# A decoder trunk on one core: q and k tokens-first, attention's operands by way of DRAM, norm's quarters in turns

## The chip, the core and the metric

One core of one Trainium2 chip runs the whole kernel as one launch. The metric is the device time of an execution in microseconds (us). The engines are PE (TensorE, matmuls and transposes), DVE (VectorE), ACT (ScalarE), POOL (GpSimd) and SP (SyncE, which here issues every DMA). The engines run their own lists of instructions in order and wait for each other by semaphores.

## The reference

```
h = RMSNorm(x);  p = h @ W_in            # x: 1024 tokens x 1024, float32
gate_pre, a_in, a_z, b_uv, b_z, q, k, v, c_z, f_pre = split(p)
A: a = GLU(a_in); causal depthwise conv, width 31; LayerNorm; silu;  a = a * silu(a_z);  y_a = a @ w_a
B: u, v = split(b_uv); v = RMSNorm(v); per group of channels tril(W_s) @ v + b_s, chunks of 128;
   y = u * mixed * silu(b_z);  y_b = y @ w_b
C: q, k = RMSNorm per head (64 wide, 8 heads); logf = log_sigmoid(f_pre + b_f); c = cumsum(logf)
   s = q k^T / 8 + c_i - c_j, causal; softmax; o = p @ v;  o = o * silu(c_z);  y_c = o @ w_c
g = sigmoid(gate_pre + b_gate)           # three of 1024 channels
out = x + (g_a*y_a + g_b*y_b + g_c*y_c) @ W_out
```

## The kernel before

Every product of float32 operands is made of three matmuls on parts: an operand is split into hi (a rounded copy) and lo (the rest), and hi·hi, lo·hi and hi·lo are added in PSUM. So each operand needs a cast (mostly ACT) and a subtraction (DVE or POOL).

The stages in order:

1. **V.** Eight tiles of 128 tokens. norm makes a tile of h, trans transposes it on PE (tile tp, line 365) and splits it (h_hi on ACT, h_lo on DVE), prod multiplies it with the weights of v and f (tiles pa and pb, lines 385 and 386) and copies the result to v and fz. The steps of the tiles are woven by hand, so that the transposes of tile i+1 stand inside the products of tile i.
2. **GLU and mixing.** Slabs of 128 output channels, features-first: slab loads 2 x 256 KB of a weight (raw), splits it (w_hi on ACT at line 147, w_lo on DVE or POOL at line 148), and gemm_steps does two halves of 512 tokens, 24 matmuls each (line 160), and hands each half's PSUM tile to an evac function. Mixing is branch B's part over tokens (lines 541 and 558).
3. **Attention.** For eight heads, scores are made per block of 128 queries (score), their weights transposed (turned) and multiplied with v (weigh). Between these small pieces stand fillers: fill(n) takes n steps from a queue of slabs. Before, the queue holds q and k of the next pair of heads (qk_steps, with the statistics matmuls at lines 206 and 207 some steps later), slabs of gates and slabs of u. ready(h) builds a head's operands from q, k and v in SBUF with casts on ACT and DVE and subtractions on POOL. The taps of branch A's convolution (tile acc, line 268) are dealt out over DVE between all this (pace and TAPS).
4. **Tail.** gated slabs (a silu gate times a branch's output, then hi and lo into br), merge slabs (merge_steps, which multiply br with w_c, w_b or w_a and with a gate gt that was stored before attention's end), branch A's LayerNorm in four quarters of 256 tokens (norm_steps), and last the product with W_out.

PE's order is the order of the code (a manual schedule for TensorE). On ACT, DVE, POOL and SP a scheduler sets the order from priorities: slab runs at raised priority, score, turned and weigh at another.

A function of another table set on ACT is preceded by an ACT_TABLE_LOAD in ACT's list.

Of the kernel before, what the change touches and what calls it, by code (L numbers as in the profile page):

```python
# [33 lines left out]
def trunk_kernel(ctx, tc, x, norm_g, w_in, b_gate, conv_w, conv_b, conv_norm_g, conv_norm_b,  # L34
# [55 lines left out]
    vo_ctx, vo = pool("vo", bufs=JC, side="right")  # L90
    vp = [vo.tile([P, NT, P], F32, name=f"v{p}", tag="vo") for p in range(JC)]
# [95 lines left out]
    def qk_steps(c0, gcol, res):  # L187
        w = slab(w2, KC, c0)
        qn = prep.tile([P, S], F32, name="qn", bufs=2)
        res.append(qn)  # L190

        def evac(hf, ps, ts):
            raw = qn[:, ts]
            sq = prep.tile([P, HALF], F32, name="sq")
            hi = prep.tile([P, HALF], F32R, name="sqhi")
            lo = prep.tile([P, HALF], F32R, name="sqlo")
            nc.scalar.copy(raw, ps)
            nc.scalar.activation(hi, ps, AF.Square)
            nc.scalar.activation(sq, ps, AF.Square)
            nc.vector.tensor_tensor(lo, sq, f32(hi), op=ALU.subtract)  # L200

            def stat():
                y0 = prep.tile([P, HALF], F32, name="y0")
                s2 = prep.tile([P, HALF], F32, name="s2")
                st = stp.tile([P, HALF], F32, name="st", tag="st")
                nc.tensor.matmul(st, lhsT=ones_hd, rhs=hi, start=True, stop=False)
                nc.tensor.matmul(st, lhsT=ones_hd, rhs=lo, start=False, stop=True)
                rsqrt(None, st, y0, s2, s2)
                nc.gpsimd.tensor_tensor(raw, raw, y0, op=ALU.mult)
                nc.vector.scalar_tensor_tensor(raw, raw, vec[:, gcol:gcol + 1], s2,  # L210
                                               op0=ALU.mult, op1=ALU.mult)

            later.append([7, stat])

        yield from gemm_steps(w, hT, evac)
# [800 lines left out]
```

## Time and profile before

| what | value |
|---|---|
| three runs | 1080.76, 1084.75 (median), 1085.66 us |
| the profiled execution | 1080.82 us, its span 1078.9 us |
| instructions | 14403 |
| PE busy | 1063.1 us, 99% of the span |
| DVE, ACT, POOL busy | 668.4, 461.1, 315.8 us |
| granted clock of TensorE | 1.00 of full speed, 0.99 in the last stage |

The span is the time between the first and the last record of the profile; the execution's time is that and what lies around it. The busy time of PE counts matmuls whose ends are modelled and overlap the next, so its share is no measure of how close PE is to its peak. What PE loses is read from its waits and from the starts of its matmuls.

### The profile page before, as it was taken

What the parts mean: (1) busy time and instruction counts of PE and PEld (TensorE: products, weight loads), DVE (VectorE), ACT (ScalarE), POOL (GpSimd) and SP (SyncE); (2) the same over time, 40 slices, a digit from 0 to 9 for tenths busy, and PEclk for the clock granted to TensorE, in tenths of its full rate; (3) what the DMA queues carried; (4) which work ended last, traced back from release to release, by engine and by line L of the source; (5) the groups of instructions that cost most, each with busy time, mean ns of one, the idle gap of its engine ahead of it and who ended that gap; (6) DMA issues with size and microseconds to landing.
All of it is one profiled execution on the core that took longest, in us unless ns stands there. A gap on an engine that the chain in (4) does not pass through costs nothing.

```text
span 1078.9 us, 14403 instructions
## 1 busy us (share of the span) xinstructions
PE 1063.1 (99%) x5256; PEld 894.9 (83%) x5256; DVE 668.4 (62%) x1233; ACT 461.1 (43%) x877; POOL 315.8 (29%) x297
## 2 busy tenths in 40 slices
PE   8999999999999899999999999999999999999998
PEld 7988888888878788888887888878888888888887
DVE  7557797878587858885788563335654355387111
ACT  6431124524366444754574444346766332365000
POOL 0022321214665646575657564201100000000000
PEclk9999999999999999999999999999999999999999
DMA  9213321023322232132222322132355233372321
GB/s 302 84 30 100 91 75 40 21 69 88 98 59 69 75 102 67 47 104 88 60 59 79 88 87 89 32 92 68 100 155 161 77 128 108 98 246 96 108 98 59
DMA packets 109443, 99.72 MB, mean 92 GB/s; under 512 B 7406, under 2 KB 82198, under 8 KB 109373
## 3 DMA queue, kind: packets, MB, share of 16 engines
q1 hardware_dynamic: 109372, 98.81, 29.9%
q8 instruction: 41, 0.67, 0.3%
q14 instruction: 30, 0.24, 0.1%
HBM read 76.21 MB, written 22.58 MB: 92 GB/s over the span
## 4 chain that ended last, share of the span: by engine, by line
PE 88%; DVE 5%; DMA 3%; ACT 1%; POOL 1%; issue 1%; SPq 0%; ACTq 0%; POOLq 0%; DVEq 0%
PE ps L160 63%; PE ops L958 8%; PE tv L541 4%; PE o L690 3%; PE tpp L670 2%; DVE acc L268 2%; PE s L647 1%; PE s L648 1%; PE pa L385 1%; PE pb L386 1%; DMA raw<-in_w_in_dram 1%; PE pm L558 1%; DVE sqlo L200 1%; DMA xt<-in_x_dram 1%; DMA mixT<-in_w_in_dram 0%
## 5 line engine op out<-in xcount | busy, mean ns | idle before, releaser
L160 PE MATMUL ps<-h_hi,w_hi 128*128 128x512 f32 x896 | 357.1, 399 | 0.9 <-DVE mixT L699 0.9
L160 PE MATMUL ps<-h_hi,w_lo 128*128 128x512 f32 x896 | 350.3, 391 | 3.3 <-POOL w_lo L148 3.3
L160 PE MATMUL ps<-h_lo,w_hi 128*128 128x512 f32 x896 | 349.6, 390 | 0.0
L268 DVE SCALAR_TENSOR_TENSOR acc<-a_in,cwT,acc 128x512 f32<-128x512 f32 x240 | 236.7, 986 | 3.8
L160 PEld LDWEIGHTS ps<-h_hi,w_lo 128*128 128x128 f32 x896 | 168.2, 188 | 40.3 <-POOL w_lo L148 3.8
L160 PEld LDWEIGHTS ps<-h_hi,w_hi 128*128 128x128 f32 x896 | 168.3, 188 | 31.2 <-ACT w_hi L147 1.3
L160 PEld LDWEIGHTS ps<-h_lo,w_hi 128*128 128x128 f32 x896 | 168.6, 188 | 30.0
L148 POOL TENSOR_TENSOR w_lo<-raw,w_hi 128x512 fp32r<-128x512 f32 x82 | 117.2, 1430 | 144.3 <-ACT w_hi L147 140.7
L147 ACT CAST w_hi<-raw 128x512 fp32r<-128x512 f32 x136 | 83.9, 617 | 143.4 <-PE ps L160 110.5
L160 PE MATMUL ps<-br,w_hi 128*128 128x512 f32 x384 | 118.3, 389 | 0.0
L676 DVE TENSOR_TENSOR plo<-tpp,phi 128x512 fp32r<-128x512 f32 (+1 forms) x80 | 50.7, 633 | 73.7 <-ACT phi L675 73.7
L160 PEld LDWEIGHTS ps<-br,w_hi 128*128 128x128 f32 x384 | 71.9, 188 | 14.7
L160 PE MATMUL ps<-br,w_lo 128*128 128x512 f32 x192 | 74.7, 389 | 0.0
L656 ACT ACTIVATE pt<-pt,nm 128x1024 f32<-128x1024 f32 (+3 forms) x64 | 49.8, 778 | 48.3 <-DVE nm L651 48.1
L148 DVE TENSOR_TENSOR w_lo<-raw,w_hi 128x512 fp32r<-128x512 f32 x54 | 37.3, 690 | 53.4 <-ACT w_hi L147 53.0
L640 POOL TENSOR_TENSOR cb<-cb,mask 128x128 f32<-128x128 f32 x64 | 44.0, 688 | 85.7 <-DVE nm L651 78.3
L659 POOL TENSOR_SCALAR pt<-pt,nm 128x1024 f32<-128x1024 f32 (+3 forms) x64 | 54.3, 848 | 49.3 <-DVE nm L658 48.9
L675 ACT CAST phi<-tpp 128x512 fp32r<-128x512 f32 (+1 forms) x80 | 43.4, 543 | 56.5 <-PE tpp L670 56.2
L966 DVE SCALAR_TENSOR_TENSOR xr<-ops,xr 128x512 f32<-128x512 f32 (+1 forms) x17 | 11.2, 660 | 72.3 <-PE ops L958 67.5
L807 ACT ACTIVATE gt<-gt,vec 128x512 f32<-128x512 f32 x46 | 32.9, 723 | 46.6 <-DMA gt<-gpre 40.4
L958 PE MATMUL ops<-wo_lo,mhi 128*128 128x512 f32 (+1 forms) x136 | 51.2, 377 | 0.0
L958 PE MATMUL ops<-wo_hi,mlo 128*128 128x512 f32 (+1 forms) x136 | 51.2, 376 | 0.0
(200 smaller groups left out, 1628.4 us busy)
## 6 DMA issues: line engine op xcount, KB each, us to landing
raw<-in_w_in_dram SPq DMA_DIRECT2D x112, 256.0 KB, 2.9
gpre<-gst SPq DMA_DIRECT2D x46, 256.0 KB, 2.0
gt<-gpre SPq DMA_DIRECT2D x46, 256.0 KB, 2.8
xt<-in_x_dram SPq DMA_DIRECT2D x8, 512.0 KB, 4.0
cb<-cT_d SPq DMA_DIRECT2D x16, 256.0 KB, 3.5
wo_raw<-in_w_out_dram SPq DMA_DIRECT2D x16, 256.0 KB, 2.7
xr<-in_x_dram SPq DMA_DIRECT2D x15, 256.0 KB, 3.7
out_dram<-xr SPq DMA_DIRECT2D x15, 256.0 KB, 2.0
```

What stands on the lines that cost most here:

```text
L147: nc.scalar.copy(hi, raw)
L148: lo_eng[0].tensor_tensor(lo, raw, f32(hi), op=ALU.subtract)
L160: nc.tensor.matmul(ps, lhsT=wk[a][:, k, :], rhs=act[b][kc][:, ts], start=kc == 0 and n == 0, stop=kc == len(w) * KH - 1 and n == 2)
L268: nc.vector.scalar_tensor_tensor(acc, a_in[:, k:k + HALF], cwT[:, j, k:k + 1], acc, op0=ALU.mult, op1=ALU.add)
L541: nc.tensor.matmul(tv, lhsT=a[:, kc, ts], rhs=b[kc][:, 0:DB], start=kc == 0 and n == 0, stop=kc == KC - 1 and n == 2)
L640: nc.gpsimd.tensor_tensor(cb[:, own], cb[:, own], mask, op=ALU.add)
L656: nc.scalar.activation(pt[:, 0:kl_], pt[:, 0:kl_], AF.Exp, bias=nm[:, ci:ci + 1], scale=-1.0, accum_out=nm[:, 2:3])
L659: ins = nc.gpsimd.tensor_scalar(pt[:, 0:kl_], pt[:, 0:kl_], nm[:, 3:4], 1.0, op0=ALU.mult, op1=ALU.mult)
L675: nc.scalar.copy(phi[:, 1:n + 1], tp[:, 0:n])
L676: ins = nc.vector.tensor_tensor(plo[:, 1:n + 1], tp[:, 0:n], f32(phi[:, 1:n + 1]), op=ALU.subtract)
L807: nc.scalar.activation(dst[hf], dst[hf], AF.Tanh, bias=bias, scale=0.5)
L958: nc.tensor.matmul(ps, lhsT=a[kc][:, ts], rhs=b[:, kc, c:c + cols], start=kc == 0 and n == 0, stop=kc == KC - 1 and n == 2)
```

## The change

- q and k are made tokens-first in 8 + 8 tiles (qk_tile) behind the first and second GLU slab: 24 matmuls into pq, RMS statistics over each head's 64 columns on ACT and DVE, the product on DVE, four transposes on PE two tiles later, hi and lo, and a store of each to DRAM. The weights of q and k are loaded and split as those of v are (weights).
- v is split in the V stage (tile vt) and stored to DRAM, one tile later than it was copied before.
- ready(h) loads a head's operands with six DMAs into tiles whose pools are open from the first stage on. It has no work on ACT, DVE or POOL.
- Attention's filler queue holds 21 gate slabs, six slabs of silu inputs (z_pre, stored to DRAM), four slabs of u and two more gates. The gaps and taps per place, and the number of score buffers (two to three), change.
- In the tail the six z slabs are read back (gated_pre, no matmuls), norm's quarters run two in turn, and merge_steps takes its weight ahead of its gate, whose tanh is issued behind the weight's cast.

```diff
-GAPS = (5, 5, 5, 5, 5, 5, 5, 5, 4, 12)
-TAPS = (3, 3, 3, 3, 2, 2, 2, 2, 0, 0)
+GAPS = (5, 5, 5, 5, 5, 6, 6, 6, 5, 5)
+TAPS = (2, 2, 2, 2, 2, 1, 1, 1, 1, 1)
-NPRE = sum(PLAN)
+NPRE = 23
+ZPRE = [(1, 0), (1, 1), (0, 0), (0, 1), (0, 2), (0, 3)]
...
-    def qk_steps(c0, gcol, res):
-        w = slab(w2, KC, c0)
...
+    def z_pre(bi, j):
+        def evac(hf, ps, ts):
+            st = prep.tile([P, HALF], F32, name="gst", bufs=2)
+            nc.scalar.copy(st, ps)
+            nc.sync.dma_start(out=zpre[bi, j][:, ts], in_=st)
+
+        yield from gemm_steps(slab(w2, KC, Z0[bi] + j * P), hT, evac)
...
+    def ready(h):
+
+        e, p = h % 2, h // 2
+        own, oth = slice(e * HD, (e + 1) * HD), slice((1 - e) * HD, (2 - e) * HD)
+        ka = stk.tile([P, S], F32R, name="ka")
+        qa = stk.tile([P, S], F32R, name="qa")
+        vc = stk.tile([P, NT, 2 * HD], F32R, name="vc")
+        with tc.high_priority(offset=PRIO):
+            for t, rows, src in ((qa, own, qk_d[0][0]), (qa, oth, qk_d[0][1]), (ka, own, qk_d[1][0]),
+                                  (ka, oth, qk_d[1][0]), (kls[e], own, qk_d[1][1])):
+                nc.sync.dma_start(out=f32(t[rows]), in_=src[own, p, :])
+            nc.sync.dma_start(out=f32(vc), in_=v_d[:, :, 2 * h * HD:2 * (h + 1) * HD])
...
-            for p in range(JC):
-                src = (pa, pb)[p // 2][:, (p % 2) * P:(p % 2 + 1) * P]
-                (nc.scalar.copy if p % 2 else nc.vector.tensor_copy)(vp[p][:, i, :], src)
+            yield
+            vt = stk.tile([P, NH, 2, HD], F32R, name="vt", tag="vc")
             nc.vector.tensor_tensor(fz[:, i, :], pb[:, N1:N1 + NH], bfb, op=ALU.add)
+            for n, src in enumerate((pa, pb)):
+                hs = slice(n * NH // 2, (n + 1) * NH // 2)
+                src = src[:, 0:N1].rearrange("p (h d) -> p h d", d=HD)
+                nc.scalar.copy(vt[:, hs, 0, :], src)
+                nc.vector.tensor_tensor(vt[:, hs, 1, :], src, f32(vt[:, hs, 0, :]), op=ALU.subtract)
+            nc.sync.dma_start(out=v_d[:, i, :], in_=f32(vt).rearrange("p h b d -> p (h b d)"))
             yield
+        def qk_tile(i, w, gcol, dst):
+
+            ts = slice(i * P, (i + 1) * P)
+            pq = ps0.tile([P, HALF], F32, name="pq", tag="pa", bufs=2)
+            for kc in range(KC):
+                for n, (a, b) in enumerate(((h_hi, w.hi), (h_lo, w.hi), (h_hi, w.lo))):
+                    nc.tensor.matmul(pq, lhsT=a[:, kc, ts], rhs=b[kc][:, 0:DC],
+                                     start=kc == 0 and n == 0, stop=kc == KC - 1 and n == 2)
+                if kc == KC // 2 - 1:
+                    yield
+            sqn = stk.tile([P, 2, NH, HD], F32, name="sqn", tag="qa")
+            sq, qn = sqn[:, 0], sqn[:, 1]
+            r = p0x.tile([P, 4, NH], F32, name="qr")
+            nc.scalar.activation(sq, pq.rearrange("p (h d) -> p h d", d=HD), AF.Square, scale=float(HD) ** -0.5)
+            nc.vector.tensor_reduce(r[:, 3], sq, axis=mybir.AxisListType.X, op=ALU.add)
+            rsqrt(r[:, 2], r[:, 3], r[:, 0], r[:, 1], r[:, 2])
+            nc.vector.tensor_tensor(qn, pq.rearrange("p (h d) -> p h d", d=HD),
+                                    r[:, 2].unsqueeze(2).broadcast_to([P, NH, HD]), op=ALU.mult)
+            yield
...
+            nc.scalar.activation(hi, tp, AF.Copy, scale=gain)
+            ins = nc.vector.scalar_tensor_tensor(lo, tp, gain, f32(hi), op0=ALU.mult, op1=ALU.subtract)
+            for t, d in zip((hi, lo), dst):
+                nc.sync.dma_start(out=d[:, :, ts], in_=f32(t))
+            pace(ins, 3)
+            yield
...
-        queue += [glu_steps(j) for j in range(JA)]
+        queue += [glu_steps(0)]
...
+        wq = weights(Q0)
...
+        fill(1000)
+        queue += [glu_steps(1)]
+        qk_tiles(wq, 36, qk_d[0])
+        wk = weights(K0)
...
+        queue += [glu_steps(j) for j in range(2, JA)]
+        qk_tiles(wk, 37, qk_d[1])
+        ready(0)
...
-        queue += [gate_pre(next(gates)) for _ in range(PLAN[1])]
-        fill(7)
-        ready(0)
-        fill(14)
+        fill(8)
         early(score, 0, 3, 1)
...
+    def gated_pre(dst, bi, j, src):
+
+        for b in dst:
+            b.append(br.tile([P, S], F32R, name="br", tag="br"))
+        for hf in range(NHALF):
+            ts = slice(hf * HALF, (hf + 1) * HALF)
+            z = zp.tile([P, HALF], F32, name="z")
+            nc.sync.dma_start(out=z, in_=zpre[bi, j][:, ts])
+            a = src(hf, ts)
+            nc.scalar.activation(z, z, AF.Silu)
+            nc.vector.tensor_tensor(a, a, z, op=ALU.mult)
+            nc.scalar.copy(dst[0][j][:, ts], a)
+            nc.vector.tensor_tensor(dst[1][j][:, ts], a, f32(dst[0][j][:, ts]), op=ALU.subtract)
...
-                nc.scalar.activation(dst[hf], dst[hf], AF.Tanh, bias=bias, scale=0.5)
+                with tc.issue_after(hi_ins[0].ins):
+                    nc.scalar.activation(dst[hf], dst[hf], AF.Tanh, bias=bias, scale=0.5)
...
     def merge_steps(bi, d, b, wm, gt=None, after=None):
+        w = slab(wm[0], len(b[0]), d * P)
...
-    queue += [gated(bb, j, BZ0, lambda hf, ts, j=j: mixT[:, j, ts]) for j in range(2)]
     queue += [merge_steps(2, d, cc, w_c) for d in range(KC)]
...
-        for q in range(S // QT):
-            for _ in norm_steps(q):
-                fill(16)
+        quarters = [norm_steps(q) for q in range(S // QT)]
+        for turn_ in ((0,), (1,), (0,), (1,), (0, 2), (1, 3), (2,), (3,), (2,), (3,)):
+            for q in turn_:
+                next(quarters[q], 0)
+            if turn_[0] < 2 and len(turn_) > 1:
+                j = turn_[0]
+                gated_pre(bb, 1, j, lambda hf, ts, j=j: mixT[:, j, ts])
+            fill(14)
```

How the lists of instructions stand in the two built programs is shown at three places. A line is source line, operation, output <- inputs and shape; lines of the changed kernel have that kernel's own line numbers.

The first place is DVE in the V stage, from the hi and lo split of a tile of h (h_lo) to the next norm's product (xt). Before:

```order
L368 TENSOR_TENSOR h_lo<-tp,h_hi 128x4x128 x2
L391 COPY v_84<-pa 128x128
L391 COPY v_86<-pb 128x128
L392 TENSOR_TENSOR fz<-pb,bfb 128x8
L121 TENSOR_TENSOR r<-r 128x1
L122 SCALAR_TENSOR_TENSOR r<-r 128x1
```

With the change:

```order
L375 TENSOR_TENSOR h_lo<-tp,h_hi 128x4x128 x2
L398 TENSOR_TENSOR fz<-pb,bfb 128x8
L403 TENSOR_TENSOR vt<-pa,vt 128x4x64
L403 TENSOR_TENSOR vt<-pb,vt 128x4x64
L125 TENSOR_TENSOR r<-r 128x1
L126 SCALAR_TENSOR_TENSOR r<-r 128x1
```

Two copies have become two subtractions on 128 x 256, and pa and pb are here those of the tile before the one that PE is at: PE's first matmul on pa of the tile after waits for the first L403, its first on pb for the second.

The second place is ACT in the tail, where the last cc slab ends (z_7196 and br_7105 before, z_7646 and br_7527 with the change are its second half; st2 is a norm quarter's statistics). Before:

```order
L790 ACTIVATE z_7196<-ps_7171 128x512
L792 CAST br_7105<-oT3_5515 128x512
L129 ACT_TABLE_LOAD
L129 ACTIVATE nsum_7237<-st2_7234,eps_111 128x256
L130 ACT_TABLE_LOAD
L130 ACTIVATE nsum_7237<-nsum_7237 128x256
L119 ACTIVATE ns2_7238<-nsum_7237 128x256
L790 ACT_TABLE_LOAD
L790 ACTIVATE z_7276<-ps_7215 128x512
```

With the change:

```order
L133 ACT_TABLE_LOAD
L133 ACTIVATE nsum_7593<-st2_7590,eps_112 128x256
L151 CAST w_hi_7785<-raw_7783 128x512
L813 ACT_TABLE_LOAD
L813 ACTIVATE z_7646<-ps_7571 128x512
L831 CAST br_7626<-mixT_80 128x512
L134 ACT_TABLE_LOAD
L134 ACTIVATE nsum_7593<-nsum_7593 128x256
L829 ACT_TABLE_LOAD
L829 ACTIVATE z_7757<-z_7757 128x512
L123 ACTIVATE ns2_7594<-nsum_7593 128x256
L815 CAST br_7527<-oT3_6358 128x512
```

The second half's Silu and cast stood ahead of the quarter's Ln and Exp; now the Ln stands ahead of the Silu, and the Exp and another Silu stand between it and the cast.

The third place is POOL in attention, where the operands of head 3 are made (qa, kl, vc) among weight parts (w_lo), masks (cb) and the scaling of scores (pt). Before:

```order
L148 TENSOR_TENSOR w_lo<-raw,w_hi 128x512
L659 TENSOR_SCALAR pt_3799<-pt_3799,nm 128x640
L609 TENSOR_TENSOR qa<-qn,qa 64x512 x2
L612 TENSOR_TENSOR kl_2490<-qn,ka 64x512 x2
L619 TENSOR_TENSOR vc<-v_85,vc 128x8x64
L640 TENSOR_TENSOR cb_4145<-cb_4145,mask 128x128
L148 TENSOR_TENSOR w_lo<-raw,w_hi 128x512
```

With the change, at the same point of a head:

```order
L701 TENSOR_SCALAR pt_4428<-pt_4428,nm 128x640
L682 TENSOR_TENSOR cb_4710<-cb_4710,mask 128x128
L152 TENSOR_TENSOR w_lo<-raw,w_hi 128x512
L682 TENSOR_TENSOR cb_4239<-cb_4239,mask 128x128
L701 TENSOR_SCALAR pt_4524<-pt_4524,nm 128x512
```

Five instructions of POOL have gone from between the scaling and the mask; their place is taken by six DMAs in SP's list.

## Rows read from the trace of the kernel before

**Rows 1.** Page, busy time: engine, us (share), slices x instructions.

```profile
PE 1063.1 (99%) x5256; PEld 894.9 (83%) x5256; DVE 668.4 (62%) x1233; ACT 461.1 (43%) x877; POOL 315.8 (29%) x297
```

**Rows 2.** Waits of PE: total us, times, longest us.

```profile
PE ps L160 <- POOL w_lo L148: 3.3, 1, 3.3
...
PE st L207 <- DVE sqlo L200: 1.8, 1, 1.8
...
PE o L690 <- DVE oT L696: 1.3, 1, 1.3
...
PE tpp L670 <- POOL pt L659: 1.2, 2, 0.7
```

**Rows 3.** Attention stage as one window: us, then PE busy (x).

```profile
256.00:714.00 458.00, 449.07 (x2295) 378.45 (x2293) 313.69 (x584) 225.19 (x442) 260.45 (x245) 1.00 0.26 76
```

**Rows 4.** Chain that ended last: start us, us, work.

```profile
153.97 5.54 PE tv L541 x24
...
807.58 180.91 PE ps L160 x798
```

**Rows 5.** Timeline of PE, 355 to 360 us: start, us, work [idle before].

```profile
355.68 0.40 PE L160 MATMUL ps<-h_lo,w_hi 128*128 128x512 f32 x1
...
359.42 0.50 PE L160 MATMUL ps<-h_hi,w_lo 128*128 128x512 f32 x1 [3.34 <-POOL w_lo L148]
```

**Rows 6.** Timeline of POOL ahead of that wait.

```profile
349.12 3.51 POOL L609 TENSOR_TENSOR qa<-qn,qa 64x512 fp32r<-64x512 f32 x2
...
357.66 3.40 POOL L148 TENSOR_TENSOR w_lo<-raw,w_hi 128x512 fp32r<-128x512 f32 x2
```

**Rows 7.** Timeline, 42 to 46 us, between two V tiles.

```profile
42.41 1.04 PE L365 MATMUL tp<-ident,xt 128*128 128x128 f32 x8
...
43.05 1.08 ACT L367 CAST h_hi<-tp 128x512 fp32r<-128x512 f32 x2 [3.35 <-PE tp L365]
...
43.20 0.36 PE L385 MATMUL pa<-wv_hi,h_hi 128*128 128x256 f32 x1
...
43.66 1.29 DVE L368 TENSOR_TENSOR h_lo<-tp,h_hi 128x512 fp32r<-128x512 f32 x2 [1.67 <-ACT h_hi L367]
...
45.46 0.28 PE L385 MATMUL pa<-wv_hi,h_hi 128*128 128x256 f32 x1
```

**Rows 8.** Groups by line and shape: xcount | busy us, mean ns | idle.

```profile
L268 DVE SCALAR_TENSOR_TENSOR acc<-a_in,cwT,acc 128x512 f32<-128x512 f32 x240 | 236.7, 986 | 3.8
...
L791 DVE TENSOR_TENSOR oT<-oT,z 128x512 f32<-128x512 f32 x8 | 6.6, 825 | 9.0 <-ACT z L790 9.0
...
L793 DVE TENSOR_TENSOR br<-oT,br 128x512 fp32r<-128x512 f32 x8 | 5.5, 692 | 4.1 <-ACT br L792 4.1
...
L864 DVE TENSOR_TENSOR nlo<-nsum,nhi 128x256 fp32r<-128x256 f32 x8 | 3.4, 420 | 0.0
...
L392 DVE TENSOR_TENSOR fz<-pb,bfb 128x8 f32<-128x8 f32 x8 | 1.3, 167 | 3.5 <-ACT v L391 3.5
...
L807 ACT ACTIVATE gt<-gt,vec 128x512 f32<-128x512 f32 x46 | 32.9, 723 | 46.6 <-DMA gt<-gpre 40.4 <-DVE gt L827 3.8 <-DVE acq L871 2.3
```

**Rows 9.** Timeline of ACT, 738 to 746 us, in the first norm quarter.

```profile
738.77 0.62 ACT L792 CAST br<-oT 128x512 fp32r<-128x512 f32 x1 [1.41 <-DVE oT L791]
739.40 1.28 ACT L129 ACT_TABLE_LOAD   x1
740.78 0.48 ACT L129 ACTIVATE nsum<-st,eps 128x256 f32<-128x256 f32 x1
741.27 1.28 ACT L130 ACT_TABLE_LOAD   x1
742.57 0.42 ACT L130 ACTIVATE nsum<-nsum 128x256 f32<-128x256 f32 x1
...
744.74 0.60 ACT L790 ACTIVATE z<-ps 128x512 f32<-128x512 f32 x1
```

**Rows 10.** Page, DMA issues: issues, KB each, us to landing.

```profile
cb<-cT_d SPq DMA_DIRECT2D x16, 256.0 KB, 3.5
```

More of the change, by code (lines that the diff above doesn't have):

```diff
@@ L89, in trunk_kernel @@
     mixT = mixp.tile([P, JB, S], F32, name="mixT")
[L90 to L91 removed]
     prep_ctx, prep = pool("prep")
     cv_ctx, cv = pool("cv")
+    stk_ctx, stk = pool("stk", bufs=2)
+    kl_ctx, klp = pool("klp")
+    kls = [klp.tile([P, S], F32R, name=f"kl{e}") for e in range(2)]
     with tc.high_priority(offset=8 * PRIO):
@@ L184, in fill @@
                     item[1]()
-    def qk_steps(c0, gcol, res):
-        w = slab(w2, KC, c0)
[L189 to L215, printed above, removed]
     PADC = KW - 1
@@ L395, in steps, with qk_tiles @@
+        def qk_tiles(w, gcol, dst):
+            g = [qk_tile(i, w, gcol, dst) for i in range(NT)]
+            for i in range(NT):
+                next(g[i])
+                if i > 1:
+                    next(g[i - 2])
+                next(g[i])
+            for gen in g[-2:]:
+                fill(9)
+                next(gen)
         def steps(*gens):
@@ L480, in trunk_kernel, with weights @@
         nc.vector.tensor_copy(cwT, pc_[:, 0:JA, 0:KW])
+        def weights(c0):
+            w = Weights(c0, DC)
+            for kc in range(KC):
+                w.high(kc)
+                w.low(kc, nc.vector if kc % 3 else nc.gpsimd)
+            return w
+        wq = weights(Q0)
         lt = [p0.tile([P, NT, NH], F32, name=f"lt{n}") for n in range(4)]
@@ L527, in trunk_kernel @@
         fill(1000)
-        gates = iter(range(NPRE))
-        queue += [qk_steps(Q0, 36, qk0), qk_steps(K0, 37, qk0)] + [gate_pre(next(gates)) for _ in range(PLAN[0])]
-        wb = Weights(BV0, DB)
-        for kc in range(KC):
-            wb.high(kc)
-            wb.low(kc, nc.vector if kc % 3 else nc.gpsimd)
+        queue += [glu_steps(j) for j in range(2, JA)]
+        qk_tiles(wk, 37, qk_d[1])
+        ready(0)
+        wb = weights(BV0)
+        fill(1000)
+        queue += [gate_pre(n) for n in range(NPRE - 2)] + [z_pre(*z) for z in ZPRE]
         def mixing(i):
@@ L692, in weigh @@
             if k2 == g:
-                own, oT = heads[h][0][3], heads[h][2]
+                own, oT = heads[h][0][3], oTs[h // 2]
                 ob = pp.tile([HD, 2 * P], F32, name="ob", bufs=2)
@@ L700, in u_slab @@
                 mixT[:, j, ts], ps, mixT[:, j, ts], op=ALU.mult))
-        oTs = []
-        qks = [qk0] + [[] for _ in range(JC - 1)]
-        def ready(h):
-            with ExitStack() as c:
-                if h == 0:
-                    c.enter_context(tc.high_priority(offset=PRIO))
-                else:
-                    c.enter_context(tc.issue_after(scaled[-1]))
-                if h % 2 == 0:
-                    oTs.append(vo.tile([P, S], F32, name=f"oT{h // 2}", tag="vo"))
-                heads[h] = [stack(h % 2, *qks[h // 2], nc.gpsimd if h else nc.vector), head_v(h), oTs[h // 2], None]
         def early(fn, *args):
@@ L748, in trunk_kernel @@
             h, at = places[n][0], n % PH
-            first = GAPS[at] // 2 if at < PH - 1 else 1
+            first = GAPS[at] // 2
             fill(first)
@@ L896, in trunk_kernel @@
     queue += [gated(bb, j, BZ0, lambda hf, ts, j=j: mixT[:, j, ts]) for j in range(2, JB)]
-    queue += [gated(ab, j, AZ0, norm_half(j)) for j in range(2)]
+    fill(1000)
+    for j in range(2):
+        gated_pre(ab, 0, j, norm_half(j))
     queue += [merge_steps(1, d, bb, w_b) for d in range(KC)]
-    queue += [gated(ab, j, AZ0, norm_half(j)) for j in range(2, JA)]
     fill(1000)
+    for j in range(2, JA):
+        gated_pre(ab, 0, j, norm_half(j))
     last = gate_tiles()
```

110 lines of the change are left out of this document (48 added, 62 removed).

## The prediction

> **What bounds the kernel now.** I read the page's busy times first. PE is busy for 1063.1 of 1078.9 us [rows 1], so there is no other engine to relieve. The change can gain only where PE waits, or by giving PE less to do. The chain that ended last says the same by stage. In the tail one unbroken run of 798 matmuls takes 180.91 us [rows 4]; that is 0.2267 us each, with nothing to gain. The waits of PE [rows 2] then list what is left. Four groups lie in attention: 3.3 us for a weight's low part from POOL, 1.8 for sqlo from DVE, 1.2 in two waits for pt from POOL, 1.3 for oT. The window of attention agrees: PE is busy for 449.07 of 458.00 us, so 8.9 us are idle there [rows 3]. That is nearly all the change could win.
>
> The largest wait shows the pattern. PE's next matmul starts 3.74 us after the one ahead of it, with 3.34 idle [rows 5]. On POOL, from 349.12 us on, stand the operands of the next head, qa first (3.51 for two), and the weight's low parts start only at 357.66 [rows 6]. A long block for the next head sits ahead of something that PE needs sooner.
>
> **The change, part by part.**
>
> *Attention gets lighter.* The operands of a head now come by six DMAs, so POOL's block and the statistics (st) of q and k leave. With them go the waits for w_lo, sqlo and pt, 3.3 + 1.8 + 1.2 = 6.3 us [rows 2]. A restart costs a little more than the idle time: 3.74 less a normal step of 0.23 is 3.51 against 3.34 [rows 4, 5], so 0.2 for each of four waits, 0.8. I take 7.1 off. The wait for oT stays in the sum: it stands behind convolution taps on DVE, which are still there, five fewer to a head. Bounds: 6.3, and 8.9 plus 1 for restarts, if all idle time goes.
>
> *PE's own work.* The st matmuls go: 32 at 0.227 us, -7.3. Transposes of q and k come: 64 at (43.20 - 42.41) / 8 = 0.099 us [rows 7], +6.3. The 384 matmuls of q and k change form; the nearest tokens-first row takes 5.54 / 24 = 0.231 [rows 4], 0.0041 more each, +1.6. Sum +0.6. The six slabs of z move from the tail into attention's filler and cost PE the same there.
>
> *Edits that I cost at nothing.* The new DMAs (32 stores of q and k, 8 of v, 6 loads a head, z both ways) lie beside PE's matmuls as long as SP issues them in time; a rival below has the price where it doesn't. Norm's quarters in turns and the tanh behind the weight's cast change no work of PE; what they change is ScalarE's order, which is costed with the tail.
>
> *The V stage.* Before, tile i was copied out after its last matmul, and DVE had nothing else to do just then. Now the hi and lo parts of tile i-1 are made behind the transposes of tile i+1 (first pair of order pieces). pa and pb have two buffers there by the waits that the program carries, so the first matmul of tile i+1 waits for DVE's subtraction on pa, the second for that on pb. I count from T, where PE resumes behind the transposes (43.20 [rows 7]). h_lo ends at 43.66 + 1.29 = 44.95, T + 1.75. Then fz, 0.17, and the subtraction on pa, nearest row nlo of the same shape at 0.42 [rows 8]: T + 2.34. The cast of pb waits for fz and ends at about T + 2.4; the subtraction on pb then ends at T + 2.85. PE wants pa at 45.46, T + 2.26 [rows 7], and pb 0.12 later. So it waits about 0.5 us in all. Five of the tile boundaries are built like this: +2.6. Bounds: 0, if the subtraction overlaps the end of h_lo; and 6.5, if the two subtractions from PSUM take twice their row, 0.8 more a tile. I take 2.6, since every term has a row.
>
> *The q and k tiles.* PE needs 24 x 0.231 + 4 x 0.099 = 5.94 us for one. DVE needs a reduction (no row; nearest a 128x512 pass, 0.69, at most a tap, 0.99), four small ones at 0.17, two passes at 0.69 to 0.83, and three taps at 0.99 [rows 8]: 5.7 to 6.3. I cost it at nothing, since pq has two buffers and the transposes come two tiles later, but that cover is thin (a rival below).
>
> *Start of attention.* The first score now stands eight filler steps behind mixing where it had 21. Its row of biases (cb) is loaded with a landing of 3.5 us [rows 10], and SP issues it only when the last mixing tile is done. Three score buffers let PE run on into the second score; it then waits some 0.5 us. Bounds 0 and 2.
>
> *The tail's turn from gates to merges.* This is the largest new cost. Before, two slabs of bb (48 matmuls each, 21.8 us together) lay between the last cc slab and merge(2, 0). Now merge(2, 0) follows directly, and it reads the last cc half, br_7527 and br_7528. Let E be the end of that slab. The merge reads the other three tiles first, and half 0 ahead of half 1, so it wants half 1 of br_7527 after 21 matmuls, E + 4.8, and br_7528 at E + 5.0 [rows 4].
>
> What ScalarE does first is in the second pair of order pieces. The Ln of the norm waits for st2, which PE ends six matmuls ahead of E, at E - 1.3. The chain ahead of it starts with z_7566 at E - 5.7 (the end of half 0), a product on DVE (0.83) and a cast (0.62), then Silu, w_hi, two tanh (0.72 each), Silu, a cast; by these rows [rows 8, 9] it reaches the first load at about E - 0.2. From there: load 1.28, Ln 0.48, w_hi 0.6, load 1.28, the Silu of half 1 0.60, a cast 0.6, load 1.28, Exp 0.42, load 1.28, Silu 0.5, Square 0.3, cast 0.62 [rows 9]. The Silu of half 1 ends at E + 4.0, its product on DVE before E + 5, but the cast of br_7527 waits in ScalarE's order until E + 9.0. On DVE br_7528 stands behind the product with z_7757 and an ns2 operation, and is done at about E + 10.0. PE waits 10.0 - 5.0 = 5.0 us. Bounds: 3.5, if ScalarE reaches the first load when st2 is there (E - 1.3) and the steps overlap fully; 7, if the z loads land late and push it. I take 5.0. Nothing absorbs it: the rest of the tail is one run of matmuls.
>
> What a change of function table costs decides this term. The row shows 1.28 us for a load; it starts at 739.40, the end of the cast before it (738.77 + 0.62), and Ln starts 0.10 behind it [rows 9], so the load's time is its row. The Trainium skill, page "ScalarE: Activation LUTs", section "What ACT_TABLE_LOAD costs", gives 1283 ns for the load and about 1380 ns of drain beside it, 2.66 us for a switch. By that figure the four loads would cost an estimated 5.5 us more and the sum would be 1087.9; no drain stands in this trace, so the measurement decides.
>
> **The sum.** The span: 1078.9 - 7.1 + 0.6 + 2.6 + 0.5 + 5.0 = 1080.5 us. Around it lie 1.9 (1080.8 against 1078.9), so 1082.4 beside the profiled execution's 1080.8. That execution lies 3.9 under the median shown (1084.75), so the same sum beside the median is 1086.3. I forecast between the two, 1084. The change takes away real waits and puts back as much: within 0.5%, 5.4 us, about what a measurement of this kernel tells from no change.
>
> **The rivals.**
>
> *More is gained than put back.* All 8.9 us of attention's idle time go, with 1.0 of restarts, since DVE and POOL have slack everywhere; the V waits are hidden; the tail's wait is at its lower bound. Span 1078.9 + 0.6 - 9.9 + 3.5 = 1073.1, so 1075 to 1079. For it: DVE's taps shared attention with POOL's blocks. Against: both new waits are worked out from rows. It decides when the two come to under 4 us together. Chance 0.27.
>
> *The q and k tiles run at DVE's pace.* At 6.3 us a tile against 5.94, 16 tiles lose 5.4 us, so 1088 to 1092, slower. It decides when DVE's work for a tile passes 5.94 us; the reduction and the taps settle that. Chance 0.12.
>
> *The long wait costs twice.* The longest wait of attention is 3.34 us [rows 5] with the granted clock at 1.00 [rows 3]. A 5 us wait has no row; if the clock then falls to the 1.2 GHz level for as long again, 5 us of work takes 10: 1089. Chance 0.09.
>
> *SP is blocked.* The loads of a head wait in SP's queue for PE to leave the tiles of two heads earlier, and the weights' loads stand behind them. If each of seven heads loses 1 to 2 us, 1091 to 1098. Against: those tiles are freed before the loads are reached by the order. Chance 0.07.
>
> *A switch of tables costs a second 1.28 us, without a row of its own.* Four loads then add 5.1: 1089. The trace's starts and ends speak against it. Chance 0.02. (This is what the Trainium skill's page "ScalarE: Activation LUTs", section "What ACT_TABLE_LOAD costs", would make of it.)
>
> **Numbers.** Within 0.5%: 0.43, the forecast. Faster: 0.27. Slower: 0.12 + 0.09 + 0.07 + 0.02 = 0.30. The range goes from 1073, under the faster case, to 1094, which leaves out the worst of the blocked queue. The forecast's own range is 1080 to 1089.
>
> **What would show it.** Attention: no wait for w_lo, sqlo or pt over 0.3 us. V stage: five waits of pa or pb for L403, about 0.5 us each. Tail: one wait of about 5 us for br at the first merge's second half, with four table loads ahead of br's cast on ACT. q and k tiles: none over 0.3 us. I am wrong if that br wait is under 3.5 us or if the q and k tiles wait for DVE's L403-like passes or taps.

## The result, and the profile after

The changed kernel takes 1097.71 us (median of 4 runs, 1094.34 to 1098.27); the kernel before took 1084.95 beside it (4 runs, 1080.76 to 1085.66). The ratio is 1.0125, with a 95% interval of 1.0108 to 1.0142: slower by 1.25%, and outside the range of 1073 to 1094. The profiled execution took 1097.99 us with a span of 1096.3, 17.4 more than the span before. The account below is of these two spans; the medians are 12.8 apart, because the profiled execution before (1080.82 us) is as fast as the fastest of the four and the one after is not.

The page after, span and busy times:

```profile
span 1096.3 us, 14672 instructions
...
PE 1074.4 (98%) x5288; PEld 902.3 (82%) x5288; DVE 618.0 (56%) x1251; ACT 435.6 (40%) x853; POOL 220.6 (20%) x247
```

PE has the 32 more instructions that were counted [rows 1]; POOL, DVE and ACT have less to do. The waits of PE after (us in total, times, longest):

```profile
PE st L905 <- ACT nhi L901: 5.0, 2, 2.8
PE ps L164 <- ACT br L815: 4.2, 1, 4.2
PE tp L372 <- DVE xt L363: 3.8, 1, 3.8
...
PE pb L393 <- DVE vt L403: 0.7, 3, 0.2
PE pb L393 <- DVE fz L398: 0.5, 2, 0.2
```

None of the four groups of [rows 2] is in this list. In their place stand four long ones that the kernel before does not have: two for nhi (the sums of the norm), one for br (the first merge's operand), one for xt (the V stage's normalized tokens). The windows tell where in the span this happens (us, then PE, PEld, DVE, ACT, POOL busy, granted clock as a share of 2.4 GHz, DMA share, GB/s):

```profile
29.10:33.20 4.10, 0.33 (x4) 0.13 (x3) 1.96 (x6) 0.62 (x1) 0.00 (x0) 1.00 0.96 325
33.20:36.00 2.80, 2.70 (x15) 2.49 (x16) 1.79 (x3) 1.77 (x3) 0.00 (x0) 0.66 0.93 318
36.00:39.00 3.00, 3.00 (x21) 3.00 (x20) 1.94 (x7) 0.95 (x4) 0.00 (x0) 0.75 0.47 171
...
310.00:770.00 460.00, 460.00 (x2365) 390.13 (x2364) 251.29 (x577) 180.78 (x375) 167.18 (x192) 1.00 0.36 102
...
829.40:833.60 4.20, 0.07 (x1) 0.00 (x0) 1.91 (x4) 4.16 (x7) 0.00 (x0) 0.91 0.48 144
833.60:840.00 6.40, 6.27 (x15) 4.62 (x16) 5.75 (x13) 5.27 (x11) 0.00 (x0) 0.53 0.25 82
840.00:849.90 9.90, 9.90 (x46) 8.09 (x44) 3.35 (x5) 4.78 (x7) 0.34 (x1) 1.00 0.68 208
849.90:853.00 3.10, 0.32 (x3) 0.06 (x1) 1.27 (x3) 3.09 (x7) 1.84 (x3) 1.00 0.33 100
853.00:858.00 5.00, 4.83 (x15) 3.79 (x16) 4.22 (x12) 4.49 (x8) 0.00 (x0) 0.66 0.46 146
...
867.20:872.00 4.80, 4.80 (x15) 3.85 (x16) 3.18 (x8) 3.46 (x8) 0.00 (x0) 0.67 0.29 88
```

The attention, 460 us of it, has no idle PE at all, where 8.9 of 458 us were idle before [rows 3]. The loss is around it. Behind each of the four waits the granted clock is between 0.53 and 0.75 for 4.8 to 6.4 us: PE is busy there, at the 1.2 GHz level for part of the stretch or nearly all of it.

The account, from these rows: attention -8.9; V stage 3.8 for xt and 1.2 for pb; br 4.2; nhi 5.0; clock behind the waits (each stretch times one minus its clock) 2.8 x 0.34 + 3.0 x 0.25 = 1.7 in the V stage and 6.4 x 0.47 + 5.0 x 0.34 + 4.8 x 0.33 = 6.3 in the tail; PE's own work +1.7 (below). Together +15.0 of the 17.4; the other 2.4 are not accounted for; restarts and short waits may hold them.

### The profile page after: what moved, and what is told of

The parts are those of the page before. It is cut to its first block, busy times and chain, and to the rows that moved or that the text cites. A ratio compares the mean times of both kernels' runs of the same rounds, so it can differ in the third digit from the quotient of the medians.

```text
span 1096.3 us, 14672 instructions
## 1 busy us (share of the span) xinstructions
PE 1074.4 (98%) x5288; PEld 902.3 (82%) x5288; DVE 618.0 (56%) x1251; ACT 435.6 (40%) x853; POOL 220.6 (20%) x247
## 5 line engine op out<-in xcount | busy, mean ns | idle before, releaser
L164 PE MATMUL ps<-h_hi,w_hi 128*128 128x512 f32 x768 | 308.7, 402 | 1.1 <-ACT gst L270 1.1
L164 PE MATMUL ps<-h_hi,w_lo 128*128 128x512 f32 x768 | 300.3, 391 | 0.0
L164 PE MATMUL ps<-h_lo,w_hi 128*128 128x512 f32 x768 | 300.2, 391 | 0.0
L241 DVE SCALAR_TENSOR_TENSOR acc<-a_in,cwT,acc 128x512 f32<-128x512 f32 x240 | 193.6, 807 | 2.6
L164 PEld LDWEIGHTS ps<-h_hi,w_lo 128*128 128x128 f32 x768 | 144.2, 188 | 32.3
L164 PEld LDWEIGHTS ps<-h_hi,w_hi 128*128 128x128 f32 x768 | 144.4, 188 | 26.3 <-ACT gst L270 1.6
L164 PEld LDWEIGHTS ps<-h_lo,w_hi 128*128 128x128 f32 x768 | 144.7, 188 | 24.8
L152 POOL TENSOR_TENSOR w_lo<-raw,w_hi 128x512 fp32r<-128x512 f32 x78 | 105.6, 1354 | 209.2 <-ACT w_hi L151 208.1
L413 PE MATMUL pq<-wv_hi,h_hi 128*128 128x512 f32 x128 | 51.3, 400 | 0.0
L1005 PE MATMUL ops<-wo_hi,mhi 128*128 128x512 f32 (+1 forms) x136 | 51.2, 376 | 0.0
```

The lines of the kernel that those rows point to most:

```text
L152: lo_eng[0].tensor_tensor(lo, raw, f32(hi), op=ALU.subtract)
L164: nc.tensor.matmul(ps, lhsT=wk[a][:, k, :], rhs=act[b][kc][:, ts], start=kc == 0 and n == 0, stop=kc == len(w) * KH - 1 and n == 2)
L241: nc.vector.scalar_tensor_tensor(acc, a_in[:, k:k + HALF], cwT[:, j, k:k + 1], acc, op0=ALU.mult, op1=ALU.add)
L413: nc.tensor.matmul(pq, lhsT=a[:, kc, ts], rhs=b[kc][:, 0:DC], start=kc == 0 and n == 0, stop=kc == KC - 1 and n == 2)
L1005: nc.tensor.matmul(ps, lhsT=a[kc][:, ts], rhs=b[:, kc, c:c + cols], start=kc == 0 and n == 0, stop=kc == KC - 1 and n == 2)
```

## The three places

**V stage, 29 to 33 us.** The timeline of DVE there (start, us, work [idle before it, releaser]):

```profile
31.14 0.69 DVE L152 TENSOR_TENSOR w_lo<-raw,w_hi 128x512 fp32r<-128x512 f32 x1 [3.37 <-ACT w_hi L151]
31.75 0.15 DVE L126 SCALAR_TENSOR_TENSOR r<-r 128x1 f32<-128x1 f32 x1
...
32.32 1.42 DVE L363 SCALAR_TENSOR_TENSOR xt<-xt,r,gb 128x512 f32<-128x512 f32 x2
```

The low part of a GLU weight (w_lo) stands in the middle of the inverse root of the fourth tile's norm, between L125 and L126 (the order of DVE shown with the change is that of a tile without it). DVE is idle for 3.37 us until the weight is there, and the norm, xt and PE's transposes wait with it. The kernel before has the same instruction on DVE too, but behind xt in the list:

```profile
26.65 1.42 DVE L356 SCALAR_TENSOR_TENSOR xt<-xt,r,gb 128x512 f32<-128x512 f32 x2
30.90 0.69 DVE L148 TENSOR_TENSOR w_lo<-raw,w_hi 128x512 fp32r<-128x512 f32 x1 [2.83 <-ACT w_hi L147]
```

It started there at 30.90 us, with the change at 31.14: the weight is about as late in both. What differs is what stands behind it.

**The first merge, 829 to 834 us.** The timeline of ACT ahead of br:

```profile
824.45 1.28 ACT L133 ACT_TABLE_LOAD   x1
825.74 0.47 ACT L133 ACTIVATE nsum<-st,eps 128x256 f32<-128x256 f32 x1
826.12 0.61 ACT L151 CAST w_hi<-raw 128x512 fp32r<-128x512 f32 x1
826.74 1.28 ACT L813 ACT_TABLE_LOAD   x1
828.04 0.60 ACT L813 ACTIVATE z<-ps 128x512 f32<-128x512 f32 x1
828.53 0.61 ACT L831 CAST br<-mixT 128x512 fp32r<-128x512 f32 x1
829.16 1.28 ACT L134 ACT_TABLE_LOAD   x1
830.46 0.42 ACT L134 ACTIVATE nsum<-nsum 128x256 f32<-128x256 f32 x1
830.89 1.28 ACT L829 ACT_TABLE_LOAD   x1
832.18 0.63 ACT L829 ACTIVATE z<-z 128x512 f32<-128x512 f32 x1
832.72 0.40 ACT L123 ACTIVATE ns<-nsum 128x256 f32<-128x256 f32 x1
833.03 0.60 ACT L815 CAST br<-oT 128x512 fp32r<-128x512 f32 x1
```

This is the list of the prediction, one by one. With PE stopping at 829.4, E (the end of the last cc slab) is 4.8 ahead, 824.6; br's cast ends at 833.63, E + 9.0, as worked out. Three of the steps (the cast at L831, a table load and a Silu at L829; 2.5 us) belong to a z slab that is read back (gated_pre).

**The norm's sums, 845 to 867 us.** The chain that ended last, in order of time (start, us, work), from the merge that frees a gate's tile to the second nhi:

```profile
844.12 2.73 DMA gt<-gpre
846.93 0.72 ACT gt L845
847.66 1.28 ACT L133
848.95 0.48 ACT nsum L133
849.49 1.26 issue
850.74 0.42 ACT nsum L134
851.16 0.52 ACT w_hi L151
...
861.27 0.51 SPq L886
861.82 4.28 DMA gt<-gpre
...
866.75 0.40 ACT nhi L901
```

The first of the two nhi waits ends behind ACT's list: a gate, two loads for Ln and Exp of another quarter, a weight's cast, another gate. In the second, nhi stands on ACT behind a gate's tanh, whose load SP issued only at 861.82, behind a load of acq (L886). Both happen while merges run, and each merge brings weights to cast and two gates to load and to turn into tanh.

## The experiments

Each is the changed kernel with the edit shown. Times are medians; ratios are to the kernel before, timed beside it.

**e1: the w_lo of the V stage taken off DVE.**

```diff
-        lo_eng[0] = nc.gpsimd if j else nc.vector
+        lo_eng[0] = nc.gpsimd
```

> The changed kernel with one line altered: the low parts of the first GLU slab's weights are made on POOL, as those of the other slabs, so that DVE's list has none of them inside the norm of a V tile. Theory 1 (the order of DVE's list made the wait of 3.8 us at 33 us, and the lower clock behind it followed from the wait): both go, about 5 us less, 1092.5 beside 1097.7. Theory 2 (the added DMA traffic makes the loads of the V stage late, whoever uses them): the wait moves to another releaser and the time stays within 1.5 us of 1097.7. Theory 3 (the clock falls by itself, not behind waits): the wait goes, 3.8 us less, and the granted clock still falls below 1.00 between 33 and 39 us.

1093.05 us, 1.0097 [1.0080, 1.0114]; the wait of tp for xt is gone (no such row; nhi 4.8 and br 4.2 stay), and the granted clock is 1.00 from 33.2 to 39 us, so theory 3 falls. The span is 4.9 shorter and the median 4.7. The ratios differ by only 0.28%, 3.0 us, since the kernel before took 1081.99 beside this run, and their intervals overlap. So the wait and the clock behind it cost 3 to 5 us, and nothing later gave that back.

**e2: branch b's last two slabs gated ahead of branch c's merges**, so that 32 steps lie between the cast of br and its use.

```diff
-            b.append(br.tile([P, S], F32R, name="br", tag="br"))
+            while len(b) <= j:
+                b.append(br.tile([P, S], F32R, name="br", tag="br"))
...
+    queue += [gated(bb, j, BZ0, lambda hf, ts, j=j: mixT[:, j, ts]) for j in range(2, JB)]
     queue += [merge_steps(2, d, cc, w_c) for d in range(KC)]
...
-    queue += [gated(bb, j, BZ0, lambda hf, ts, j=j: mixT[:, j, ts]) for j in range(2, JB)]
-    fill(1000)
     for j in range(2):
         gated_pre(ab, 0, j, norm_half(j))
```

> The changed kernel with the slabs of bb[2] and bb[3] moved ahead of the first merge, so that 21.8 us of matmuls lie again between the last cc slab and merge(2, 0). Theory 1: the wait for br (4.2 us) goes with the lower clock behind it (3.1 us), and the norm's loads (acq) no longer stand behind gate loads in SP's queue, so the two waits for nhi (5.0 us, with 3 us of lower clock) go too: 16 us less, about 1082. If only the first belongs to the order and the nhi waits are the pairing of the quarters: 7.5 less, about 1090. Theory 2 (traffic): the waits move, the time stays above 1094.

1102.47 us, 1.0187 [1.0167, 1.0207]: slower. The waits of PE, first three rows:

```profile
PE ps L164 <- ACT br L833: 6.8, 1, 6.8
PE st L908 <- ACT nhi L904: 6.3, 2, 4.7
PE tp L372 <- DVE xt L363: 4.1, 1, 4.1
```

The wait at the first merge is gone, but another br wait came later (branch b's first slabs, whose tiles come free only when branch c's merges are done: a flaw of the edit), and the nhi waits grew. The expected gain did not come. The nhi waits end at 849.9 and 864.0 us, long before the one that the flaw made (912.5), so the flaw is not their cause. Ahead of the second, ACT is idle for the load of a z slab that is read back inside the norm's turns, and nhi stands behind that slab's Silu:

```profile
863.01 0.63 ACT L831 ACTIVATE z<-z 128x512 f32<-128x512 f32 x1 [3.51 <-DMA z<-zpre]
863.54 0.69 ACT L904 CAST nhi<-nsum 128x256 fp32r<-128x256 f32 x2
```

**e3: the quarters one by one, in 8 turns of 16 steps.**

```diff
-        quarters = [norm_steps(q) for q in range(S // QT)]
-        for turn_ in ((0,), (1,), (0,), (1,), (0, 2), (1, 3), (2,), (3,), (2,), (3,)):
-            for q in turn_:
-                next(quarters[q], 0)
-            if turn_[0] < 2 and len(turn_) > 1:
-                j = turn_[0]
-                gated_pre(bb, 1, j, lambda hf, ts, j=j: mixT[:, j, ts])
-            fill(14)
+        for q in range(S // QT):
+            for _ in norm_steps(q):
+                fill(16)
+            if q < 2:
+                gated_pre(bb, 1, q, lambda hf, ts, j=q: mixT[:, j, ts])
```

> The changed kernel with the norm's quarters one after the other with 16 filler steps a turn, as before; the rest as changed. If the pairing of quarters made the two waits for nhi: they go, 8 to 9 us less, about 1089, and the wait for br stays or changes with ScalarE's order. If they come from SP's queue, where the next quarter's loads stand behind gate loads that wait for a merge: nhi waits stay, more of them, since more turns now fall beside merges: 1095 to 1105.

1093.85 us, 1.0108 [1.0093, 1.0123]. The br wait shrinks to 0.8, the nhi waits stay at 6.0 with one of 5.7. That one has only 30 matmuls ahead of it: the queue ran dry in the last turn, because 6 + 8 x 16 = 134 steps are asked of 128. The time lies between the two that were expected: the nhi waits neither went nor became more.

**e4: three edits together** (e1, e2, and in the V stage the evacuations ahead of the transposes):

```diff
-   steps(ns[i + 1], ps_[i], ps_[i], ts_[i + 1], ts_[i + 1], *([ps_[i - 1]] if i > 2 else []), ps_[i])
+   steps(ns[i + 1], *([ps_[i - 1]] if i > 2 else []), ps_[i], ps_[i], ts_[i + 1], ts_[i + 1], ps_[i])
```

> The first two edits together, and V's copy out made ahead of the next tile's transposes in place of behind them. Theory 1: all new waits go, the V stage's four of 0.45 us too, and what attention won stays (about 9 us): 1097.7 - 5 - 16 - 2 = about 1075, 0.9% under the kernel before. Theory 2: over 1085. Theory 3 (the clock falls whatever the waits): 1080 to 1084, with a granted clock under 0.998 over the span.

1096.21 us, 1.0133 [1.0117, 1.0148]. The waits for xt and vt are gone; br 7.5 and nhi 6.9 remain, as in e2, and the expected 1075 is missed. The theory that the tail needs only another order of the same steps had missed twice. The next four runs part V stage from tail.

**e5: the two V-stage edits alone** (e1 and the last line of e4).

> Two edits in the V stage alone: the low parts of the first GLU slabs are formed on POOL again (as in the kernel before), and the evacuations of the V accumulators stand ahead of the next tile's transposes. Theory 1 (each wait of TensorE costs its own length plus the lower granted clock behind it, and nothing downstream makes it up): the changed kernel's 1097.7 less 4.9 (the run with the first edit alone) less 1.0 to 2.2 (the waits of pb for vt and fz, 0.46 us each): 1090.5 to 1092. Theory 2 (what is won ahead of the attention is lost again at later waits, because transfers or ACT set the times there): the waits of the tail grow by the same amount and the time stays at 1094 to 1098.

1090.46 us, 1.0078 [1.0060, 1.0096]: theory 1. (One parenthesis of the expectation is wrong: the kernel before forms that w_lo on DVE as well; only its place in DVE's list differs.) By the ratios of e1 and e5 the evacuations alone cost about 2 us, by the medians 2.6; the intervals of e1 and e5 overlap. The two V windows:

```profile
29.10:33.20 4.10, 4.00 (x34) 3.74 (x33) 2.65 (x4) 2.77 (x6) 1.29 (x1) 1.00 1.02 387
33.20:44.00 10.80, 10.80 (x93) 10.80 (x92) 7.05 (x20) 4.37 (x12) 0.95 (x1) 1.00 0.43 151
```

Without the wait, the clock does not fall.

**e6: more steps between the norm's turns**, by queueing branch b's gating and merges behind branch c's.

```diff
     queue += [merge_steps(2, d, cc, w_c) for d in range(KC)]
+    queue += [gated(bb, j, BZ0, lambda hf, ts, j=j: mixT[:, j, ts]) for j in range(2, JB)]
+    queue += [merge_steps(1, d, bb, w_b) for d in range(KC)]
...
-            fill(14)
-
-
-    fill(1000)
+            fill(17)
...
-    queue += [gated(bb, j, BZ0, lambda hf, ts, j=j: mixT[:, j, ts]) for j in range(2, JB)]
-    fill(1000)
...
-    queue += [merge_steps(1, d, bb, w_b) for d in range(KC)]
```

> The tail alone: the steps that stand between the norm's turns are more (the gating of branch b's last two slabs and branch b's merges are queued behind branch c's merges from the start, the turns are 17 steps in place of 14, and the queue is not emptied before the second branch). On ACT's list the cast of the last cc slab now stands ahead of the first table load of the norm. Theory 1 (the cost of the tail is the norm's chain, too long for its turns and in front of the cast for the first merge, with the clock behind each wait): the br wait (4.4 and 3.1 of clock) and the nhi waits (6.1 and 3 of clock) go or shrink to under 3 us in all: 1081 to 1086. Theory 2 (ACT's work in the tail as a whole is too much for TensorE's rate there, so a wait comes back wherever the order puts it): the nhi and br waits move, their sum stays above 6 us, and the time is 1092 to 1098.

1094.97 us, 1.0111 [1.0096, 1.0127]. The br wait at the first merge is gone, since its cast now stands ahead of the table loads. But nhi (3.9, longest 3.4) and br at a later merge (2.8 and 1.1) wait: theory 2, the waits move.

**e7: e5 and e6 together.**

> The edits of the two runs beside it together (both of the V stage, and the longer queue of the tail). Theory 1 (the losses are separate, and the attention's gain of about 10 us is kept): the sum of both, 6 to 7 and 12 to 16 us under the changed kernel's 1097.7, so 1075 to 1080, and below the kernel before (1082 to 1085). Theory 2 (something that all parts share, such as the transfers' 34 MB more, bounds the kernel): no lower than 1085, with new waits for transfers.

1087.70 us, 1.0045 [1.0028, 1.0062]. The two add up, but the tail still has 4.6 us of nhi and 3.8 of br, so the 1075 to 1080 is missed; theory 2 fails too, since none of the longer waits is for a transfer.

**e8: e7 with the quarters one by one**, `fill(20)` in 8 turns.

> As the run with both edits, but the norm's quarters one after the other as in the kernel before, in 8 turns of 20 steps. Theory 1 (what matters is how much work stands between two steps of a quarter, not whether quarters take turns): within 3 us of the run with turns, 1075 to 1081, nhi waits under 2 us. Rival (interleaving is what hides the chain; one by one, each step of a quarter stands close behind the one before, and Ln, Exp and Silu of one quarter delay the sums of the next): nhi waits of 5 us or more as in the run with quarters one by one and 16 steps, so 1082 or more.

1086.87 us, 1.0034 [1.0021, 1.0047]. No nhi wait is left, and the time is within 3 us of e7 as theory 1 had it, but its 1075 to 1081 is missed: now the first merge waits 1.5 us for br, and a product with h later in the tail 3.5 for its w_hi. In each order of the same steps that was tried the tail's wait came back, at br, nhi or w_hi. So no order tried was enough. Before the change, two more slabs of products (32 steps, 21.8 us) lay between the gating of branch c and its merges: products that need only h, which is long there, and one weight each. The change had put them into the attention's filler, in the place that the q and k products left there.

**e9: those products given back to the tail**, on top of e5; the gaps of attention then have 5 steps each, and the two slabs' loads and Silus (gated_pre) leave the norm's turns.

```diff
-GAPS = (5, 5, 5, 5, 5, 6, 6, 6, 5, 5)
+GAPS = (5, 5, 5, 5, 5, 5, 5, 5, 5, 5)
-ZPRE = [(1, 0), (1, 1), (0, 0), (0, 1), (0, 2), (0, 3)]
+ZPRE = [(0, 0), (0, 1), (0, 2), (0, 3)]
...
+    queue += [gated(bb, j, BZ0, lambda hf, ts, j=j: mixT[:, j, ts]) for j in range(2)]
     queue += [merge_steps(2, d, cc, w_c) for d in range(KC)]
...
-            if turn_[0] < 2 and len(turn_) > 1:
-                j = turn_[0]
-                gated_pre(bb, 1, j, lambda hf, ts, j=j: mixT[:, j, ts])
```

> On top of the two V-stage edits (that run alone: 1090.5), the gating of branch b's first two slabs is a product in the tail again, queued between branch c's gating and its merges as in the kernel before: 32 more steps of 0.68 us between them. They no longer stand in the attention's queue, whose gaps are 5 steps each throughout in place of 5 or 6. The norm's quarters still take turns. Theory 1 (the tail lost its cover because the change took those products out of it to fill the attention, where the q and k products had stood): the br wait and the nhi waits with their clock, some 15 us in the run with the V-stage edits, fall under 3 us; the attention loses 0 to 4 us through the smaller gaps; 1075 to 1081. Rival (the norm's turns and the gates' loads on SP's queue are enough by themselves): br wait gone, nhi waits of 4 us or more with the clock behind them, 1082 to 1087.

1076.31 us, 0.9931 [0.9910, 0.9951]: faster than the kernel before. No br wait, nhi and nlo 0.6 and 0.5.

The 32 steps are not all that came back. e2 had 32 steps of the same kind at the same place, and its nhi waits stayed at 6.3. What e2 kept, and e9 takes out, is gated_pre of branch b's first two slabs: four loads of z, four Silus and their casts on ACT among the norm's steps. So e9 shows that the two slabs belong in the tail. How much of the gain comes from the steps, and how much from ACT's shorter list, no run parts.

**e10: e9 with the quarters one by one, 16 steps each.**

> As the run beside it, but the norm's quarters one by one in 8 turns of 16 steps, as in the kernel before. Theory 1 (cover is what counts): within 3 us of the run with turns, 1075 to 1081, no nhi wait over 1 us. Rival (turns are the fault): clearly better than the run with turns, by 4 us or more.

1073.95 us, 0.9909 [0.9892, 0.9927], the best of all. The two longest waits of PE, both at the start, then attention and the tail to 880 us as windows:

```profile
PE wu L472 <- DVE wz L462: 1.5, 1, 1.5
PE pa L392 <- ACT wv_hi L342: 1.0, 1, 1.0
```

```profile
310.00:745.00 435.00, 435.00 (x2250) 369.14 (x2249) 250.54 (x569) 173.73 (x362) 164.14 (x188) 1.00 0.37 103
745.00:829.00 84.00, 83.46 (x376) 69.12 (x375) 45.66 (x89) 53.24 (x94) 10.78 (x12) 1.00 0.37 109
829.00:880.00 51.00, 51.00 (x228) 42.31 (x227) 24.51 (x47) 27.65 (x47) 0.00 (x0) 1.00 0.51 156
```

The attention stays free of idle time with smaller gaps, and the tail to 880 us has 0.5 us of idle time in all. The turns themselves cost about 2.4 us here (e9 less e10) and gain nothing. The span is 1072.2 us, 6.7 under that of the profiled execution before; the medians are 9.4 apart. The clock over the span is 1.000 in all four executions here and 0.995 to 0.998 in the seven of the kernel before beside them.

**e11: e7 with the loads of acq issued by POOL** in place of SP.

> The run with the V-stage edits and the long queue (1087.7) with one edit: the loads of the norm's quarters are issued by POOL, which sums them, and no longer stand behind the gates' loads on SP's queue. If the nhi waits (4.6 us and the clock behind them) come from loads that SP issues late behind gate loads that wait for a free tile, they fall under 1.5 us and the time is 1080 to 1084. If they come from ACT's list (Ln, Exp, Silu of one quarter ahead of the sums of the next) or from the two buffers of acq, they stay, and so does the time, 1086 to 1089.

1090.84 us, 1.0072 [1.0048, 1.0095]. nhi still waits 4.5 us, longest 3.4, and the time is above both ranges: that loads of acq behind gate loads make the nhi waits falls, in the order of e7. The gates' loads themselves stayed on SP's queue, so they are not cleared by this run.

**e12: the cover given back alone** (e9 without the V-stage edits).

> The changed kernel with only the cover of the tail given back (gating of branch b's first two slabs as products in the tail, gaps of 5 in the attention); the V stage stays as changed. If the losses of V stage and tail are separate: the run with the V-stage edits too (1076.3) plus what these edits gave by themselves (1097.7 less 1090.5, 7.2): 1083 to 1085, no different from the kernel before; the tp wait for xt (2.6 to 3.9 us) and the pb waits (0.46 us each) are there, the br wait and the nhi waits over 1 us are not. If the tail's waits depend on how the stages before it stand in time, it comes out 3 us or more from that.

1083.50 us, 0.9995 [0.9985, 1.0005]: no difference from the kernel before. The first and fourth of PE's waits:

```profile
PE tp L372 <- DVE xt L363: 4.2, 1, 4.2
...
PE pb L393 <- DVE vt L403: 0.7, 3, 0.2
```

From the changed kernel to here is 1.0125 - 0.9995 = 1.3%, 14 us: the tail. From here to e9 is 0.64%, 7 us: the V stage. The losses are separate and add up.

## Why the prediction was wrong

*Attention.* Predicted -7.1, measured -8.9: all idle time went, as in the bound of 8.9 plus 1 for restarts (what restarts gave is not read here). No wait for w_lo, sqlo or pt is left, nor one for oT, which I had kept.

*PE's own work.* The count is right (+32). At a clock of 1.000 in both profiles, PE is busy for 1064.8 us in e10 and for 1063.1 before [rows 1]: +1.7, where the sum had +0.6. Which of its terms is off is open.

*q and k tiles, start of attention, SP in attention.* The products of q and k, costed at nothing, have no idle time ahead of them (last column; the other two forms, lo with hi and hi with lo, show 0.0 as well):

```profile
L413 PE MATMUL pq<-wv_hi,h_hi 128*128 128x512 f32 x128 | 51.3, 400 | 0.0
```

So the rival of tiles at DVE's pace (16 tiles at 0.36 are 5.8, not the 5.4 of its sum) fell, and so did that of a blocked SP where it was put, in attention; the 0.5 at its start did not come either. That the measured 1097.71 lies in the 1091 to 1098 of the blocked queue is chance: the attention, where that rival put its cost, has no idle time.

*V evacuations.* Five short waits of pb at the named place, none of pa, each 0.24 us long where about 0.5 was worked out: 1.2 idle. Predicted +2.6 (five times 0.5 is 2.5), and 2 to 2.6 by e1 and e5, so the total fits better than its parts do.

*The br wait.* Predicted 5.0 with a list of 12 steps on ACT; measured 4.2 idle, by the same list. The first term that was put on the path in the tail was right, and so were the four table loads: each takes 1.28 us, with what stands behind it 0.01 to 0.02 later. The rival of a second 1.28 a switch finds no support: this trace shows no drain beside these loads. The Trainium skill's page "ScalarE: Activation LUTs", section "What ACT_TABLE_LOAD costs", gives about 1380 ns of drain beside the load.

*The step that failed* is the one by which edits were costed at nothing: "Norm's quarters in turns and the tanh behind the weight's cast change no work of PE; what they change is ScalarE's order, which is costed with the tail", with the sentence that the six slabs of z cost PE the same in attention's filler. PE's own work agrees (+1.7 in all). But in the tail two of them had been the cover of the norm's chain, of the casts and of the gates (work that PE could do meanwhile), and reading them back put loads and Silus into the norm's turns. I priced this at one place, the first merge, and followed ACT's list to the end of that cast; the same list goes on into two nhi waits, 5.0 us more, and the clock fell behind all three. e12 shows what the two slabs are worth in the tail: given back, 14 us. That cover alone does it is not shown; e2 speaks against it for the nhi waits.

*The second miss* is in the V stage's term. I followed evacuations only. DVE's list there also holds the GLU weight's low part, moved from behind xt into the middle of the norm, and it waits for a transfer: 3.8 us of idle time, and 3 to 5 with its clock (e1).

*The third* is the clock. "The long wait costs twice" was a rival at 0.09, for one wait. The clock did fall, behind all four, but no wait cost twice: 3.0 us are lost behind the 4.2 of br, 1.7 behind the 3.8 of xt, and 1.7 and 1.6 behind the nhi waits. Together that is 8.0 us by the windows (1.7 and 6.3).

With what was measured in each term's place, the predicted span of 1080.5 becomes 1080.5 - 1.8 (attention) + 1.1 (PE's work) - 1.4 (V evacuations, idle time alone) - 0.5 (start) - 0.8 (br) = 1077.1, and the three misses of 5.0, 3.8 and 8.0 make it 1093.9; 1096.3 was measured. The terms that were worked out were off by little; the 16.8 us that were not in the sum decide.

## What to carry to other kernels

Matmuls moved to fill a gap are cover taken from where they stood: before costing the move at nothing, list what they hid there, on every engine, to the end of the stage and not to the first wait. In each engine's list, look for the instruction that waits for a transfer and ask what now stands behind it; one row in the middle of a norm cost 3 to 5 us, a good part of the attention's gain of 8.9. Price also what moved work leaves behind: a result that is read back later brings its loads and its Silu into the list of another engine. And where several orders of the same steps each bring the wait back at another place, try giving the stage its independent work back; here that was worth 14 us.
